# Attention rows of one core: transposing by pairs of heads over two key tiles, into wide tiles, with four pairs of row buffers

## The chip, the core and the metric

The kernel runs on one core of a Trainium2 chip, in one launch. The metric is the device time of that launch in microseconds (us). The kernel before takes 1777.0 us, the median of three runs (1774.48 to 1779.74).

## What is computed

Two layers of a diffusion backbone over 512 latent tokens and 256 context tokens of width 1024. Layer 0 is windowed attention with 16 query heads and 4 key heads of 64, layer 1 is retention; each is followed by a gated feed-forward part. The change touches the attention of layer 0 alone. Cut to what matters, for each block `b` of 128 latent queries:

```python
s_ctx = einsum('bqkgd,bnkd->bkgqn', qb, k_c) * scale           # 256 context keys
s_loc = einsum('bqkgd,bnkd->bkgqn', qb, kb) * scale            # keys within 128 of the query
s_loc = where(valid, s_loc, NEG_INF)
p = softmax(concatenate([s_ctx, s_loc, sink_col], -1))
o = einsum('bkgqn,bnkd->bqkgd', p[..., :L], v_c) + einsum('bkgqn,bnkd->bqkgd', p[..., L:L+band], vb)
out_x = o @ w_o
```

The context queries attend in the same way, to the context keys alone.

## The kernel before

Everything is fp32. Large products are made of three fp32r products each (`mm3`, lines 148 to 150). The attention of layer 0 is a double loop (lines 787 to 797): over the four groups `g` of one key head and four query heads, and inside over six blocks, the latent blocks 0 to 3 and the context blocks 0 and 1. A block is a call of `attend` and does this:

- `score(i)`, once for each of the four heads. PE multiplies 128 queries with the block's keys into a bank of PSUM (line 684; three banks). DVE adds the mask, writes the *row tile* `pr` (128 queries by up to 640 keys and one sink column) and keeps the row's extreme (line 685). POOL has written the sink column (line 668), which is the first write to that row tile. After the second head of a pair DVE makes the two biases (691), ACT the two exponentials with their sums (101), DVE the reciprocals (695), and POOL scales the two row tiles (698).
- `turn(ki)`, once for each key tile of 128 keys (4, 5, 5, 4 tiles for the latent blocks, 2 for a context block). PE transposes that tile of all four heads into one of two PSUM banks `pT` (707), in the order of heads 0, 2, 1, 3. ACT copies it to a tile `tt` of 512 columns where `ki` is even, DVE where it is odd (709).
- `output()`. For each key tile two products of the values with 256 columns of `tt` (719). Its first product waits for the block's last copy, so that all run together. The result goes to `o_raw` (734) or, in the last group, is split into `h` tiles (165, 166).

There are seven row buffers (`PRB`), and six buffers of `tt` (`TTB`). Before the loop both are also used in making the keys: `kn` (line 513) are `tt` tiles, `ksq` and a temporary of `key_factor` are `pr` tiles, and `rope_key` (520) takes one more `tt`.

Between the blocks of one group the query projections of the next are made (`make_q`, called in line 791); they are 96 products per pair of heads that depend on no softmax. After the loop come the output weights (`wo`, lines 809 to 824): each tile of 1024 weights is loaded, split by ACT into `whi` (140) and by DVE into `wlo` (141), and multiplied. The first two output tiles need only latent blocks.

The order in which the instructions stand in each engine's queue is not the program's. Outside the stretches under `manual_schedule` a scheduler decides it when the kernel is built: it takes what its own model holds ready, and by the program's order between those. On the chip each engine then works through its fixed queue. POOL's queue holds lines 668, 698 and 570 (a step of `make_q`), SP's the loads.

Of the kernel before, what the change touches and what calls it, by code (L numbers as in the profile page):

```python
# [14 lines left out]
P = 128  # L15
# [26 lines left out]
N_SMALL = C_C + 16  # L42

NM = 7
PRB = 7
TTB = 6


@with_exitstack
def dit_kernel(ctx, tc, xT, cT, crow, small, consts, masks, tabs0, tabs1, jtab, adaQ, adaN, adaT, wst, out):  # L50
    nc = tc.nc
# [10 lines left out]
    def T(pool, cols, tag, bufs, dt=F32):  # L62
        return pool.tile([P, cols], dt, tag=tag, bufs=bufs, name=tag)
# [8 lines left out]
    ident, bd = cst[:, 0:128], cst[:, 128:256]  # L72
# [16 lines left out]
    turn = {"pre": None, "lnexp": [], "silu": []}  # L89
# [418 lines left out]
    ap = At.enter_context(tc.tile_pool(name="ap", bufs=1, reuse_waits="tile"))  # L508
# [1 line left out]


    kx, kc = {}, {}
    kn = [T(ap, 512, "tt", TTB) for _ in range(3)]
    ksq = [T(ap, 656, "pr", PRB)[:, :512] for _ in range(3)]
    off_grid(ap, 16)
    for a, b, o in zip(kn, ksq, (kvx[0], kvc, kvx[1])):
# [2 lines left out]

    def rope_key(t):  # L520

        yy = T(ap, 512, "tt", TTB)
        nc.vector.stream_shuffle(yy, t, swap16)
        nc.vector.tensor_tensor(t, t, rope0[:, 0:512], op=mult)
        nc.vector.tensor_tensor(yy, yy, rope0[:, 512:1024], op=mult)
        nc.vector.tensor_tensor(t, t, yy, op=add)
# [18 lines left out]
    q, stats = {}, {}  # L545

    def make_q(j, raw=None):

        w = next_w(ap, 1, raw)
        qs = T(ap, 64, "qs", 4)[:, 0:36].rearrange("p (f n) -> p f n", f=3)
        sqs, o = [], [None, None]

        def part(s, k0, k1):
            if k0 == 0:
                o[s] = pj(NTOK[s])
            for k in range(k0, k1):
                mm3(o[s], (w[0][:, k * P:(k + 1) * P], w[1][:, k * P:(k + 1) * P]), h[s][k], k == 0, k == KT - 1)

        def shape(s):
            n = NTOK[s]
            sq, qn = t_sq(n), t_hn(n)
            nc.scalar.activation(qn, o[s], AF.Identity, scale=qk_gain[:, 0:1])
            nc.scalar.activation(sq, o[s], AF.Square)
            sqs.append(sq)
            if s == 0:
                sw = t_y(s)
                nc.vector.stream_shuffle(sw, qn, swap16)
                nc.gpsimd.tensor_tensor(qn, qn, rope0[:, 0:512], op=mult)  # L570
                nc.vector.tensor_tensor(sw, sw, rope0[:, 512:1024], op=mult)
                nc.vector.tensor_tensor(qn, qn, sw, op=add)
            qa = T(ap, 512, "q", 9, F32R)
            if s == 0:
                qb = T(ap, 512, "q", 9, F32R)
            else:
                qa, qb = qa[:, 0:SC], qa[:, SC:2 * SC]
            nc.scalar.copy(qa[0:64, :], qn[0:64, :])
            nc.scalar.copy(qb[64:128, :], qn[64:128, :])
            nc.vector.tensor_tensor(qa[64:128, :], qn[0:64, :], qa[0:64, :], op=sub)  # L580
            nc.vector.tensor_tensor(qb[0:64, :], qn[64:128, :], qb[64:128, :], op=sub)
            q[2 * j, s] = qa
            q[2 * j + 1, s] = qb

        def norms():
            tot = pj(12)
            for s, sq in enumerate(sqs):
                for b in range(NTOK[s] // P):
                    c = 8 * s + 2 * b
                    nc.tensor.matmul(tot[:, c:c + 2], sq[:, b * P:(b + 1) * P], bd[:, 0:P:64], start=True, stop=True)  # L590
            y, u, z = qs[:, 0], qs[:, 1], qs[:, 2]
            neg_half_rstd(y, z, tot, HD)
            nc.vector.scalar_tensor_tensor(u, tot, HD * EPS, y, add, mult)
            ue = u.rearrange("p (b e) -> p e b", e=2)
            for e in range(2):
                hd = 2 * j + e
                nc.vector.tensor_scalar(ue[:, e], ue[:, e], nsink[:, hd:hd + 1], -4.0 / HD, op0=mult, op1=mult)
                stats[hd] = qs

        def first():  # L600
            part(0, 0, 5)

        def second():
            part(0, 5, KT)
            shape(0)
            part(1, 0, 3)

        def third():
            part(1, 3, KT)
            shape(1)  # L610

        return [first, second, third, norms]
# [36 lines left out]
    class Block:  # L649


        def __init__(self, g, s, b):
            self.g, self.s, self.b = g, s, b
            self.lk = list(range(max(0, b - 1), min(4, b + 2))) if s == 0 else []
            ck = [4, 5]
            self.keys = ck + self.lk if s == 0 and b == 3 else self.lk + ck
            self.pr = []

        def score(self, i):
            g, s, b, n = self.g, self.s, self.b, len(self.keys) * P  # L660
            hd, nl = 4 * g + i, len(self.lk) * P
            if i % 2 == 0:
                self.st = T(ap, 16, "stat", 4)
            st, c = self.st, 2 * (b + 4 * s)
            qt = q[hd, s][:, b * P:(b + 1) * P]
            pt = T(ap, 656, "pr", PRB)[:, :n + 1]
            top = stats[hd][:, 1, c + hd % 2:c + hd % 2 + 1]
            nc.gpsimd.tensor_copy(pt[:, n:n + 1], top)
            lo, x0 = st[:, i % 2:i % 2 + 1], self.lk[0] * P if nl else 0

            if nl == 384:
                runs = [(nl, SC, 5 * P, [(0, SC, kc)]), (0, nl, 2 * P, [(0, nl, kx)])]
            elif nl == 0:
                runs = [(0, SC, 5 * P, [(0, SC, kc)])]
            elif b == 0:
                runs = [(0, n, 3 * P, [(0, nl, kx), (nl, SC, kc)])]
            else:
                runs = [(0, n, 0, [(0, SC, kc), (SC, nl, kx)])]
            for c0, w, m0, parts in runs:
                bank = pS()[:, :w]  # L680
                for p0, pw, kk in parts:
                    for r in range(2):
                        keys = kk[g][r] if kk is kc else kk[g][r][:, x0:x0 + pw]
                        nc.tensor.matmul(bank[:, p0:p0 + pw], qt, keys, start=r == 0, stop=r == 1)  # L684
                nc.vector.tensor_tensor_reduce(pt[:, c0:c0 + w], bank, mask[:, m0:m0 + w], 1.0, top, add, ALU.min, lo)  # L685
                top = lo
            self.pr.append(pt)
            if i % 2 == 0:
                return
            y = stats[hd][:, 0, c:c + 2]  # L690
            nc.vector.scalar_tensor_tensor(st[:, 2:4], st[:, 0:2], -1.0, y, mult, mult)  # L691
            for e in range(2):
                pt = self.pr[i - 1 + e]
                lnexp(pt, pt, AF.Exp, scale=y[:, e:e + 1], bias=st[:, 2 + e:3 + e], accum_out=st[:, 4 + e:5 + e])
            nc.vector.reciprocal(st[:, 6:8], st[:, 4:6])  # L695
            for e in range(2):
                pt = self.pr[i - 1 + e]
                nc.gpsimd.tensor_scalar(pt[:, :n], pt[:, :n], st[:, 6 + e:7 + e], 1.0, op0=mult, op1=mult)  # L698
            if i == 3:
                self.tt = []  # L700

        def turn(self, ki):
            if ki >= len(self.keys):
                return
            tp = pT()
            for a in range(4):
                nc.tensor.transpose(tp[:, a * P:(a + 1) * P], self.pr[(0, 2, 1, 3)[a]][:, ki * P:(ki + 1) * P], ident)  # L707
            tt = T(ap, 512, "tt", TTB)
            self.last = nc.scalar.copy(tt, tp) if ki % 2 == 0 else nc.vector.tensor_copy(tt, tp)
            self.tt.append(tt)  # L710

        def output(self):
            g, s, b = self.g, self.s, self.b
            O = pO()[:, :256]
            for ki, (t, tt) in enumerate(zip(self.keys, self.tt)):
                vg = vt[t][:, g * HD:(g + 1) * HD]
                f, l = ki == 0, ki == len(self.keys) - 1
                for e in range(2):
                    ins = nc.tensor.matmul(O[64 * e:64 * e + 64, :], vg, tt[:, 256 * e:256 * e + 256], start=f, stop=l)  # L719
                    if f:  # L720
                        tc.add_manual_dep(ins.ins, self.last.ins.name, run_dep, reason="value products in one run")
            if g == NKV - 1:
# [10 lines left out]
            dst = o_raw[g, s, b // 2].rearrange("p (e b q) -> p e b q", e=2, b=2)[:, :, b % 2, :]  # L733
            nc.vector.tensor_copy(dst, O.rearrange("p (e q) -> p e q", e=2))

    def attend(g, s, b):
        blk = Block(g, s, b)
        for i in range(4):
            blk.score(i)
        for ki in range(len(blk.keys)):  # L740
            blk.turn(ki)
        blk.output()

    def split_o(g):
# [65 lines left out]
    for d4 in range(0, KT, 4):  # L810
# [3 lines left out]
        for s, res in ((0, xr), (1, cres)):  # L814
            for d in range(d4, d4 + 4):
                o = pj(NTOK[s])
                project(w[d - d4], o_t[s], o)
                ins = gated_add(s, 0, 2, d, o, res)
# [236 lines left out]
    f, prev = 0, None  # L1055
    for gsz in FFN_GROUPS:
        acts = []
        for i in range(gsz):
# [4 lines left out]
            else:  # L1063
                if f == PLAIN:
                    last_sum()
                a, end = seven()
# [563 lines left out]
    f, prev = 0, None  # L1630
# [160 lines left out]
```

## Time and profile before

| what | value |
|---|---|
| median of three runs | 1777.0 us (1774.48 to 1779.74) |
| profiled execution | 1777.24 us, span of its instructions 1775.5 us |
| PE, DVE, ACT, POOL busy in the span | 97%, 76%, 47%, 8% |
| granted TensorE clock, mean | 0.994 |
| stage of the attention blocks | about 102 to 326 us |

The profiled execution's own time is 1.7 us over its span and 0.2 us over the median. "Busy" of PE counts matmuls whose ends are modelled, and they overlap, so that a short wait may not show as idle time. In the lists below a line reads: group, count, busy time, mean duration in ns, then the idle time of the engine just before the group and what ended it. A line of the timeline reads: start, duration, engine, source line, operation, tiles, shape, count, and in brackets the idle time before it with what ended it.

### The profile page before, as it was taken

How to read it: one execution, taken by the hardware profiler on the slowest of the kernel's cores; microseconds unless marked ns; L12 is line 12 of the kernel's file. 1: busy time of each engine (PE TensorE's matmuls, PEld its weight loads, DVE VectorE, ACT ScalarE, POOL GpSimd, SP SyncE). 2: the span in 40 equal slices, each digit the busy share in tenths (PEclk: the TensorE clock that was granted, in tenths of full speed). 3: DMA queues.
4: the chain of work that ended last, by engine and by line, in shares of the span. 5: the costliest groups of instructions: out<-in, count | busy, mean ns of one | idle time of the engine just before them, and what ended most of it. 6: DMA issues, size and time to landing. Idle time of an engine off the chain costs nothing.

```text
span 1775.5 us, 27602 instructions
## 1 busy us (share of the span) xinstructions
PE 1717.1 (97%) x10852; PEld 1527.1 (86%) x10852; DVE 1356.0 (76%) x2365; ACT 841.2 (47%) x1477; POOL 134.4 (8%) x275
## 2 busy tenths in 40 slices
PE   6899999999999999999998999999999999999999
PEld 4777776789999999999978788898897899999998
DVE  6697786788778778777789758758758798777774
ACT  5477676456333434242465534524524564445432
POOL 0035344100000000000010000000000000000000
PEclk9999999999999999999999999999999999999999
DMA  8610002434243534343342534434433323333222
GB/s 334 239 36 25 25 1 84 145 107 165 73 154 107 157 116 143 119 146 111 123 133 88 164 106 132 153 102 132 153 104 119 95 72 116 94 112 107 92 88 83
DMA packets 59891, 206.68 MB, mean 116 GB/s; under 512 B 6641, under 2 KB 7025, under 8 KB 59505
## 3 DMA queue, kind: packets, MB, share of 16 engines
q1 hardware_dynamic: 52848, 179.75, 31.2%
q0 software_dynamic: 6912, 25.17, 4.8%
q8 instruction: 85, 1.39, 0.3%
q14 instruction: 46, 0.37, 0.1%
HBM read 202.80 MB, written 2.10 MB: 115 GB/s over the span
## 4 chain that ended last, share of the span: by engine, by line
PE 74%; DVE 13%; ACT 4%; DMA 4%; issue 2%; POOL 2%; SPq 0%; ACTq 0%; DVEq 0%; POOLq 0%
PE Y L835 13%; PE Z L835 6%; PE pj L148 6%; PE pj L150 6%; PE pj L149 6%; PE Y L1180 4%; PE Z L1193 3%; PE X L835 3%; DVE wlo L166 3%; DMA wraw<-in_wst_dram 2%; PE pT L707 2%; PE S L684 2%; PE pO L719 2%; PE pj L1193 2%; PE X L1180 1%
## 5 line engine op out<-in xcount | busy, mean ns | idle before, releaser
L165 ACT CAST whi<-wraw 128x1024 fp32r<-128x1024 f32 x177 | 185.5, 1051 | 305.3 <-PE Z L150 71.5
L166 DVE TENSOR_TENSOR wlo<-wraw,whi 128x1024 fp32r<-128x1024 f32 x177 | 215.7, 1221 | 42.1 <-ACT whi L165 41.6
L835 PE MATMUL Y<-aq,whi 128*128 128x384 f32 x640 | 173.7, 335 | 0.9 <-ACT hn L973 0.8
L253 DVE SCALAR_TENSOR_TENSOR res<-pj,mod,res 128x512 f32<-128x512 f32 (+1 forms) x112 | 81.6, 729 | 70.3 <-PE pj L150 69.1
L141 DVE TENSOR_TENSOR wlo<-wraw,whi 128x1024 fp32r<-128x1024 f32 x80 | 97.9, 1223 | 36.6 <-ACT whi L140 36.0
L140 ACT CAST whi<-wraw 128x1024 fp32r<-128x1024 f32 x80 | 84.0, 1050 | 75.9 <-DMA wraw<-in_wst_dram 26.8
L835 PEld LDWEIGHTS Y<-aq,whi 128*128 128x128 f32 x640 | 116.6, 188 | 2.4 <-ACT hn L973 2.0
L271 DVE CUSTOM_DVE_ANT_0 y<-adaw,crow,small_sb 128x1024 bf16<-128x1024 f32 x64 | 81.9, 1279 | 33.7 <-DMA adaw<-in_adaT_dram 33.5
L835 PE MATMUL Y<-aq,wlo 128*128 128x384 f32 x320 | 107.0, 334 | 0.0
L101 ACT ACTIVATE pr<-pr,stat,qs 128x513 f32<-128x513 f32 (+2 forms) x96 | 74.2, 775 | 30.7 <-DVE stat L691 29.8
L1193 PE MATMUL Z<-whi,sA 128*128 128x512 f32 x256 | 81.0, 392 | 0.6 <-ACT whi L165 0.6
L698 POOL TENSOR_SCALAR pr<-pr,stat 128x512 f32<-128x512 f32 (+2 forms) x96 | 68.0, 721 | 86.7 <-DVE stat L695 66.6
L148 PE MATMUL pj<-ax,whi 128*128 128x512 f32 x176 | 68.7, 390 | 1.0 <-DVE res L253 1.0
L150 PE MATMUL pj<-ax,whi 128*128 128x512 f32 x176 | 68.6, 390 | 0.0
L149 PE MATMUL pj<-ax,wlo 128*128 128x512 f32 x176 | 68.5, 389 | 0.0
L707 PE MATMUL pT<-const_sb,pr 128*128 128x128 f32 x352 | 58.0, 284 | 10.9 <-POOL pr L698 8.6
L148 PE MATMUL pj<-act,whi 128*128 128x512 f32 x168 | 66.0, 393 | 0.1
L149 PE MATMUL pj<-act,wlo 128*128 128x512 f32 x168 | 65.9, 392 | 0.0
L707 PEld LDWEIGHTS pT<-const_sb,pr 128*128 128x128 f32 x352 | 38.8, 140 | 31.3 <-POOL pr L698 19.2
L150 PE MATMUL pj<-act,whi 128*128 128x512 f32 x168 | 65.5, 390 | 0.0
L268 POOL DMA_DIRECT2D adaw<-in_adaT_dram x48 | 25.6, 533 | 520.6 <-DVE mod L271 420.8
L685 DVE CUSTOM_DVE_ANT_0 pr<-S,mask,qs 128x256 f32<-128x256 f32 (+1 forms) x96 | 53.1, 567 | 14.3 <-PE S L684 7.9
(518 smaller groups left out, 5273.7 us busy)
## 6 DMA issues: line engine op xcount, KB each, us to landing
wraw<-in_wst_dram SPq DMA_DIRECT2D x238, 512.0 KB, 3.6
adaw<-in_adaT_dram POOLq DMA_DIRECT2D x48, 512.0 KB, 3.9
wx<-in_wst_dram SPq DMA_DIRECT2D x24, 512.0 KB, 4.6
adan<-in_adaQ_dram SPq DMA_DIRECT2D x16, 512.0 KB, 8.0
adan<-in_adaN_dram SPq DMA_DIRECT2D x16, 512.0 KB, 8.5
res<-in_xT_dram SPq DMA_DIRECT2D x16, 256.0 KB, 5.5
adaw<-in_adaT_dram SPq DMA_DIRECT2D x8, 512.0 KB, 4.0
aq<-in_adaN_dram SPq DMA_DIRECT2D x12, 256.0 KB, 6.4
```

The costliest lines, as they stand in the source:

```text
L140: nc.scalar.copy(hi, raw)
L141: nc.vector.tensor_tensor(lo, raw, hi, op=sub)
L148: nc.tensor.matmul(o, whi, xhi, start=first, stop=False)
L149: nc.tensor.matmul(o, wlo, xhi, start=False, stop=False)
L150: return nc.tensor.matmul(o, whi, xlo, start=False, stop=last)
L165: nc.scalar.copy(hi, t)
L166: return nc.vector.tensor_tensor(lo, t, hi, op=sub)
L271: after(nc.vector.tensor_tensor_reduce(junk, w, cr[:, s * 1024:(s + 1) * 1024], 1.0, sm_t[:, C_ADAB + l * 48 + j:C_ADAB + l * 48 + j + 1], ...
L707: nc.tensor.transpose(tp[:, a * P:(a + 1) * P], self.pr[(0, 2, 1, 3)[a]][:, ki * P:(ki + 1) * P], ident)
L835: nc.tensor.matmul(o, p, r, start=first and k + i == 0, stop=k == 3 and i == 2, skip_group_check=not first)
L1180: ins = nc.tensor.matmul(o[:, e * SC:(e + 1) * SC], p[:, ws], r, start=first and k + e + i == 0, stop=k == 3 and i == 2, skip_group_check= ...
L1193: ins = nc.tensor.matmul(o, p, r, start=first and k + i == 0, stop=k == 3 and i == 2, skip_group_check=not first)
```

## The change

`turn` takes two key tiles and two heads at a time instead of one key tile and four heads; `tt` tiles are 1024 columns wide, three of them instead of six of 512; there are eight row buffers instead of seven.

- A wide tile holds two key tiles of all four heads: the first pair of heads in its left half, the second pair in its right half. `turns` goes over the first pair with all whole pairs of key tiles, then over the second pair. Where the number of key tiles is odd, the last one is turned for all four heads together as before.
- The copy of the 1st, 3rd bundle of a pair of heads is ACT's, that of the 2nd DVE's, and the odd last tile's ACT's. Over all blocks ACT has 56 copies instead of 48, DVE 32 instead of 40. Counts of transposes (352), value products (176), row tiles (96) and POOL's scalings (96) stay.
- `moving` picks from a wide tile the 256 columns of a key tile and a head of each pair: two runs of 128 columns that lie 512 apart. Before they were 256 columns in a row.
- `kn` are the left halves of the three wide tiles; the temporary of `rope_key` becomes a row buffer. A tile `qs` shrinks from 64 to 48 columns.

```diff
-PRB = 7
-TTB = 6
+PRB = 8
+TTB = 3
...
-    kn = [T(ap, 512, "tt", TTB) for _ in range(3)]
+    kn = [T(ap, 1024, "tt", TTB)[:, :512] for _ in range(3)]
...
     def rope_key(t):
-        yy = T(ap, 512, "tt", TTB)
+        yy = T(ap, 656, "pr", PRB)[:, :512]
...
-        def turn(self, ki):
-            if ki >= len(self.keys):
-                return
+        def turn(self, kis, heads, eng):
             tp = pT()
-            for a in range(4):
-                nc.tensor.transpose(tp[:, a * P:(a + 1) * P], self.pr[(0, 2, 1, 3)[a]][:, ki * P:(ki + 1) * P], ident)
-            tt = T(ap, 512, "tt", TTB)
-            self.last = nc.scalar.copy(tt, tp) if ki % 2 == 0 else nc.vector.tensor_copy(tt, tp)
-            self.tt.append(tt)
+            for i, (ki, hd) in enumerate((ki, hd) for ki in kis for hd in heads):
+                nc.tensor.transpose(tp[:, i * P:(i + 1) * P], self.pr[hd][:, ki * P:(ki + 1) * P], ident)
+            while len(self.tt) <= kis[0] // 2:
+                self.tt.append(T(ap, 1024, "tt", TTB))
+            dst = self.tt[kis[0] // 2][:, heads[0] * 256:heads[0] * 256 + 512]
+            self.last = nc.scalar.copy(dst, tp) if eng == 0 else nc.vector.tensor_copy(dst, tp)
+
+        def turns(self):
+            n = len(self.keys)
+            for p in range(2):
+                for ki in range(0, n - 1, 2):
+                    self.turn((ki, ki + 1), (2 * p, 2 * p + 1), ki // 2 % 2)
+            if n % 2:
+                self.turn((n - 1,), (0, 1, 2, 3), 0)
+
+        def moving(self, ki, e):
+            n, t = len(self.keys), self.tt[ki // 2]
+            if n % 2 and ki == n - 1:
+                return t[:, 0:512].rearrange("p (j e q) -> p e j q", j=2, e=2)[:, e]
+            return t.rearrange("p (j k e q) -> p k e j q", j=2, k=2, e=2)[:, ki % 2, e]
...
-                    ins = nc.tensor.matmul(O[64 * e:64 * e + 64, :], vg, tt[:, 256 * e:256 * e + 256], start=f, stop=l)
+                    ins = nc.tensor.matmul(O[64 * e:64 * e + 64, :], vg, self.moving(ki, e), start=f, stop=l)
...
-        for ki in range(len(blk.keys)):
-            blk.turn(ki)
+        blk.turns()
```

The scheduler places all instructions of the stage anew. On PE the queue is the same up to the first transposes and again from the last value product on; ACT's, DVE's and POOL's come together again there. On SP the load of one tile of output weights moves from before the twelve loads of the residual streams to behind them.

More of the change, by code (lines that the diff above doesn't have):

```diff
@@ L551, in make_q @@
         w = next_w(ap, 1, raw)
-        qs = T(ap, 64, "qs", 4)[:, 0:36].rearrange("p (f n) -> p f n", f=3)
+        qs = T(ap, 48, "qs", 4)[:, 0:36].rearrange("p (f n) -> p f n", f=3)
         sqs, o = [], [None, None]
@@ L656, in __init__ @@
             self.keys = ck + self.lk if s == 0 and b == 3 else self.lk + ck
-            self.pr = []
+            self.pr, self.tt = [], []
         def score(self, i):
@@ L698, in score @@
                 nc.gpsimd.tensor_scalar(pt[:, :n], pt[:, :n], st[:, 6 + e:7 + e], 1.0, op0=mult, op1=mult)
-            if i == 3:
-                self.tt = []
-        def turn(self, ki):
-            if ki >= len(self.keys):
-                return
-            tp = pT()
-            for a in range(4):
-                nc.tensor.transpose(tp[:, a * P:(a + 1) * P], self.pr[(0, 2, 1, 3)[a]][:, ki * P:(ki + 1) * P], ident)
-            tt = T(ap, 512, "tt", TTB)
-            self.last = nc.scalar.copy(tt, tp) if ki % 2 == 0 else nc.vector.tensor_copy(tt, tp)
-            self.tt.append(tt)
+        def turn(self, kis, heads, eng):
+            tp = pT()
+            for i, (ki, hd) in enumerate((ki, hd) for ki in kis for hd in heads):
[16 more added lines that the diff above has]
+            return t.rearrange("p (j k e q) -> p k e j q", j=2, k=2, e=2)[:, ki % 2, e]
         def output(self):
@@ L714, in output @@
             O = pO()[:, :256]
-            for ki, (t, tt) in enumerate(zip(self.keys, self.tt)):
+            for ki, t in enumerate(self.keys):
                 vg = vt[t][:, g * HD:(g + 1) * HD]
```

## The prediction

> **What bounds the kernel now.** I read the page first, then the busy times by stretch.
>
> ```profile
> span 1775.5 us, 27602 instructions
> PE 1717.1 (97%) x10852; PEld 1527.1 (86%) x10852; DVE 1356.0 (76%) x2365; ACT 841.2 (47%) x1477; POOL 134.4 (8%) x275
> ```
> ```profile
> 102.00:326.00 224.00, 210.28 (x1445) 162.47 (x1444) 172.94 (x543) 152.49 (x360) 91.81 (x199) 1.00 0.11 37
> 326.00:1775.00 1449.00, 1426.26 (x8522) 1298.78 (x8522) 1116.00 (x1663) 636.43 (x1020) 38.32 (x65) 0.99 0.38 119
> ```
>
> PE bounds the program. The change lies in the first stretch, where PE is idle for 224.0 - 210.3 = 13.7 us (columns: stretch, length, then PE, PEld, DVE, ACT, POOL). Behind it PE is 98% busy and the queues are the same in both kernels, so what the stage gains or loses reaches the end. The list of waits in this stage says what PE waits for, and what waits for PE (us in total, times, longest):
>
> ```profile
> POOL pr L668 <- PE pT L707: 29.2, 18, 3.5
> ...
> PE pT L707 <- POOL pr L698: 8.6, 14, 1.2
> ...
> PE pT L707 <- ACT tt L709: 1.3, 4, 0.4
> ```
>
> Two thirds of PE's idle time stands before a transpose whose row tile POOL has not scaled yet. And 18 times POOL's first write to a row tile waited for transposes: with seven buffers, the fourth head of a block reuses one of the block before, and all four heads' buffers are freed by the last key tile. One such loop, at the fourth latent block of group 2, in the timelines of PE, POOL and DVE:
>
> ```profile
> 252.39 0.91 PE L707 MATMUL pT<-const_sb,pr 128*128 128x128 f32 x5
> ...
> 252.86 0.54 POOL L668 COPY pr<-qs 128x1 f32<-128x1 f32 x4 [1.55 <-PE pT L707]
> ...
> 252.87 0.75 DVE L685 CUSTOM_DVE_ANT_0 pr<-S,mask,qs 128x512 f32<-128x512 f32 x1
> ...
> 254.57 1.77 DVE L571 TENSOR_TENSOR y<-y,rope 128x512 f32<-128x512 f32 x1
> ...
> 257.87 0.15 DVE L695 RECIPROCAL stat<-stat 128x2 f32<-128x2 f32 x1
> ...
> 258.12 1.88 POOL L698 TENSOR_SCALAR pr<-pr,stat 128x512 f32<-128x512 f32 x2 [2.33 <-DVE stat L695]
> ...
> 258.96 0.55 PE L707 MATMUL pT<-const_sb,pr 128*128 128x128 f32 x3 [1.13 <-POOL pr L698]
> ```
>
> The last transposes of one block at 252.4 let the fourth row of the next be written at 252.9; its scaling comes at 258.1, and PE stands still.
>
> **The change part by part.** *The loop goes.* With eight buffers a block's rows reuse those of the block before last, and a first pair is freed before the second. Of the 14 waits, four are not of the loop (their fourth row was written before the other heads' work was through, or there was no block before):
>
> ```profile
> 112.36 0.44 PE L707 MATMUL pT<-const_sb,pr 128*128 128x128 f32 x2 [0.42 <-POOL pr L698]
> ...
> 195.40 0.55 PE L707 MATMUL pT<-const_sb,pr 128*128 128x128 f32 x3 [0.20 <-POOL pr L698]
> ...
> 272.29 0.66 PE L707 MATMUL pT<-const_sb,pr 128*128 128x128 f32 x4 [1.23 <-POOL pr L698]
> ...
> 322.22 1.11 PE L707 MATMUL pT<-const_sb,pr 128*128 128x128 f32 x6 [0.39 <-POOL pr L698]
> ```
>
> 8.6 - (0.42 + 0.20 + 1.23 + 0.39) = 6.4 us may go: I take -6.4. The bounds are 0 (the reciprocal of the example also stood behind other DVE work) and -8.6.
>
> *A first pair of heads gets a wait of its own.* Before, the first transposes of a block needed heads 0 and 2 and the rest all four; now 24 blocks have two such points each. In the built queue of the second latent block of groups 1 and 2 there stand, between the last scores of head 1 and that pair's first transposes, the scores of two heads, eight transposes, eight value products and four projection products. Rows of these kinds, and the chain of a pair of 640 columns (mean ns behind the bar's comma):
>
> ```profile
> 289.75 0.48 PE L684 MATMUL S<-kc,q 128*128 128x256 f32 x2
> ...
> 290.43 0.39 PE L684 MATMUL S<-kc,q 128*128 128x256 f32 x2
> ...
> 292.09 0.40 PE L148 MATMUL pj<-h,whi 128*128 128x512 f32 x1
> ...
> 292.33 0.40 PE L149 MATMUL pj<-h,wlo 128*128 128x512 f32 x1
> ...
> 294.87 1.04 PE L707 MATMUL pT<-const_sb,pr 128*128 128x128 f32 x8
> ...
> 297.78 2.38 PE L719 MATMUL pO<-tt,v 128*64 128x256 f32 x20
> ```
> ```profile
> L101 ACT ACTIVATE pr<-pr,stat,qs 128x641 f32<-128x641 f32 x32 | 29.4, 920 | 21.7 <-DVE stat L691 21.6
> ...
> L698 POOL TENSOR_SCALAR pr<-pr,stat 128x640 f32<-128x640 f32 x32 | 26.9, 853 | 40.4 <-DVE stat L695 26.3 <-DVE stat L691 14.1
> ...
> L685 DVE CUSTOM_DVE_ANT_0 pr<-S,mask,qs 128x256 f32<-128x256 f32 x64 | 29.8, 478 | 10.1 <-PE S L684 5.4 <-PE pT L707 4.3
> ...
> L685 DVE CUSTOM_DVE_ANT_0 pr<-S,mask,stat 128x384 f32<-128x384 f32 x32 | 19.2, 606 | 0.7 <-PE S L684 0.2
> ```
>
> PE's cover, from start to start since matmuls overlap (a head's scores run from its context product to the next head's), is 2 x (290.43 - 289.75) + 1.04 + 8 x 2.38 / 10 (a value product is two instructions, so x20 are ten) + 4 x (292.33 - 292.09) = 5.3 us. The chain is 0.48 + 0.61 for the mask, 2 x 0.92 for the exponentials, 2 x 0.85 for the scalings and about 0.3 for biases and reciprocal (0.15 each, as at 257.87): 4.9 us, without any queue on the way. So the new points are tight, and queues make some of them wait. Queued behind a waiting transpose is all of PE. No row shows such a point; the nearest are the old ones, 8.6 / 24 = 0.36 us for a block. 24 new ones would cost 8.6; a second pair is scored ahead of the first pair's transposes, so a wait for the first lets the second run on, and I take half: +4.3 (0 to +8.6).
>
> *The end of the stage.* The last head of the last context block, before (PE, DVE and POOL):
>
> ```profile
> 317.15 0.48 PE L684 MATMUL S<-kc,q 128*128 128x256 f32 x2
> ...
> 318.24 0.47 DVE L685 CUSTOM_DVE_ANT_0 pr<-S,mask,qs 128x256 f32<-128x256 f32 x1
> ...
> 321.36 0.15 DVE L695 RECIPROCAL stat<-stat 128x2 f32<-128x2 f32 x1
> ...
> 321.69 0.93 POOL L698 TENSOR_SCALAR pr<-pr,stat 128x256 f32<-128x256 f32 x2 [3.56 <-DVE stat L695]
> ...
> 324.20 1.08 PE L719 MATMUL pO<-tt,v 128*64 128x256 f32 x8 [0.88 <-ACT sq L209]
> ...
> 326.59 0.80 PE L148 MATMUL pj<-h,whi 128*128 128x512 f32 x1 [1.30 <-ACT whi L140]
> ```
>
> In the built queues of the change no copy of DVE stands ahead of this mask, the reciprocal stands ahead of the splits, and four projection products stand between the last transposes and the value products, where PE now idles 0.88 us for the copy. I take 0.9 for the copy, and 0.9 for mask and reciprocal (the mask begins 318.24 - 317.63 = 0.6 after the scores' end): -1.8, bounds 0 and -2.5. The 1.30 us before the next product stays: ACT splits those weights behind the block's result in both queues.
>
> *Banks.* Four waits of 1.3 us for a bank's copy: bundles of one pair come with other work between in the last blocks; half, -0.7 (bounds -1.3 and 0).
>
> *The clock.* PE's granted clock falls once in the stage. Stretches of 3.41 us there, and elsewhere (the last three numbers are clock, DMA share and GB/s):
>
> ```profile
> 323.13:326.54 3.41, 1.28 (x10) 0.57 (x8) 1.68 (x3) 2.24 (x5) 0.00 (x0) 1.00 1.01 412
> 326.54:329.95 3.41, 3.04 (x6) 2.11 (x7) 2.56 (x3) 3.38 (x5) 0.00 (x0) 0.50 0.89 292
> 329.95:333.37 3.42, 3.42 (x9) 2.65 (x8) 1.29 (x2) 2.29 (x3) 0.00 (x0) 0.50 0.64 247
> 903.40:906.80 3.40, 1.62 (x14) 1.42 (x13) 3.40 (x7) 2.21 (x5) 1.51 (x2) 1.00 0.25 55
> 906.80:910.20 3.40, 2.51 (x10) 1.76 (x11) 3.40 (x5) 1.04 (x3) 1.75 (x1) 1.00 0.54 146
> ```
>
> After 1.28 us of work in 3.41 the clock is halved for 6.8 us; after 1.62 it is not. Half of 3.04 + 3.42 is 3.2; less 0.3 for waits that would show again, 2.9. Without the 0.88 before the value products a stretch there keeps 1.28 + 0.88 = 2.2 us of work, over 1.62: I take -2.9 (bounds 0 and -3.2). The Trainium skill's page "TensorE: Matmul & The Clock Gate", section "What's actually happening", has the clock halved after at least one idle window of about 3.4 us. The row at 323.13 differs, since PE worked in it. By the rule alone this fall would not hang on the 0.88 us, and the sum would lack this term: 1772.4.
>
> *What costs nothing.* Eight copies go from DVE to ACT, which is idle for a third of the stage. The value products read two runs of 128 columns instead of one of 256; two products of 256 columns (0.39 at 290.43) take no longer than one of 512 (0.40 at 292.09), so not even a new start shows: 0, and no gain is possible as the columns are the same. The load that moves behind twelve others on SP brings weights that are split only at the stage's end; cover lost, it would add to the wait at 326.59. POOL's queue keeps its instructions, in another order. The keys' temporaries end before the first scores, under projections.
>
> The sum: -6.4 + 4.3 - 1.8 - 0.7 - 2.9 = -7.5, on the profiled execution's 1777.24 us: 1769.7. The median lies 0.2 lower: **1769.5 us**.
>
> **The rivals.** *The waits change place.* What the loop gives back, the first pairs take (+6.4 instead of +4.3), and the clock falls as before: -1.8 - 0.7 - 0.2 = 1774.3. For it: cover 5.3 against chain 4.9. Against: 18 blocked writes go for certain. Chance 0.28.
>
> *Slower: POOL stays late, and is asked twice.* DVE's addition at 254.57 took 1.77 us and POOL's two scalings of 512 columns 1.88, while two engines were at work on the same memory. If rows come as late as now because of that, nothing of the 8.6 goes, the 24 new points cost their 8.6 in full, and the end gains 1.8: 1777.0 + 6.8 = 1783.8. It decides from where the first pairs' waits pass 6.4 + 5.3 us. For it: only 4 of 24 blocks are in the loop with more than 1 us. Chance 0.22. The Trainium skill's page "SBUF — State Buffer", section "Who interferes with whom", speaks for it: a DVE operation with two SBUF inputs and POOL exclude each other for a whole instruction.
>
> *Slower: wide tiles run out.* A block of five key tiles holds all three, the old six buffers left one. At the two changes to a next block of four or five key tiles in each group, PE would wait for a bank for about a copy and half a bundle of eight (0.59 as ACT's tt copies, 1.04 / 2): 8 x 1.1 = 8.8, less 2.5: 1783.3. It needs transposes of the next block ahead of this block's value products; the built queue has them behind. Chance 0.05.
>
> ```profile
> L709 ACT COPY tt<-pT 128x512 f32<-128x512 f32 x48 | 28.1, 585 | 28.6 <-PE pT L707 28.1
> ```
>
> **How the numbers follow.** The forecast has 0.45, the rivals 0.28, 0.22 and 0.05. 0.3%, about what a measurement of this kernel can tell from no change, is 5.3 us: below 1771.7 or above 1782.3. The forecast is faster, the first rival within, the others slower: 0.45, 0.28, 0.27. The forecast's own range goes from all of 8.6, 2.5, 1.3 and 3.2 gained, cut by 5 for first pairs that must wait somewhere, 1766, to no gain of the clock, 1772.4. If first pairs never wait it is near 1761. The range of 8 in 10 reaches from 1760 to 1784.
>
> **What would show it.** Right: POOL's writes at L668 no longer wait for transposes; PE's waits for POOL total 4 to 7 us, at twice as many points; the value products of the last block wait for nothing; the clock stays at 1.00 around 326 us. Wrong: waits for POOL over 12 us, above all before first pairs; PE waiting for copies by more than 3 us; a stage that ends at 326 or later.

## The result, and the profile after

The changed kernel takes 1769.0 us, the median of 6 executions (1767.17 to 1771.39), against 1776.7 us before (6 executions): a ratio of 0.9952, 95% interval 0.9941 to 0.9963. The forecast was 1769.5. Two of the 6 stand on record with the same time, span and clock (1767.17 us), as if one execution had been listed twice; counted once, the median is 1769.9. The profiled execution took 1767.17 us, with a span of 1765.4 us.

From the page of the changed kernel, and the busy times by stretch (stretch, length, then PE, PEld, DVE, ACT, POOL; the last three numbers are granted clock, DMA share and GB/s):

```profile
span 1765.4 us, 27623 instructions
PE 1713.7 (97%) x10852; PEld 1526.2 (86%) x10852; DVE 1347.7 (76%) x2357; ACT 845.4 (48%) x1485; POOL 139.0 (8%) x275
```
```profile
102.00:326.00 224.00, 214.14 (x1463) 166.87 (x1462) 167.78 (x539) 161.44 (x374) 95.39 (x196) 1.00 0.14 46
326.00:1765.00 1439.00, 1417.49 (x8498) 1292.34 (x8496) 1112.10 (x1658) 631.42 (x1013) 38.70 (x65) 1.00 0.38 118
```

PE has as much to do as before. In the first 224 us of the stage it idles 9.9 us where it idled 13.7, and has got 18 instructions further. The list of waits in the stage, as shown of before, with three lines added that matter now (us in total, times, longest):

```profile
POOL pr L668 <- PE pT L704: 22.7, 23, 1.7
...
PE pT L704 <- POOL pr L698: 3.8, 10, 1.0
...
PE pj L148 <- ACT whi L140: 2.0, 2, 1.4
PE pT L704 <- DVE tt L708: 2.0, 2, 1.0
...
DVE pr L685 <- PE pT L704: 0.9, 2, 0.4
```

And the same line of before as the last one:

```profile
DVE pr L685 <- PE pT L707: 5.9, 8, 0.9
```

PE's waits for POOL fall from 8.6 to 3.8 us. The waits for a bank's copy were 1.3 us, on ACT; now they are 2.0 us, on DVE. POOL's first writes to row tiles (668) still wait for transposes, 23 times instead of 18: that sign was read wrongly. What has all but gone (5.9 us to 0.9) is the wait behind them, that of a mask (685) for a row tile that transposes still held.

The end of the stage, in PE's timeline after, and below it one row of before that stands for the same product as the last of after:

```profile
316.70 1.08 PE L731 MATMUL pO<-tt,v 128*64 128x256 f32 x8
319.18 0.49 PE L148 MATMUL pj<-h,whi 128*128 128x512 f32 x1 [1.40 <-ACT whi L140]
320.29 0.50 PE L148 MATMUL pj<-h,whi 128*128 128x512 f32 x1 [0.62 <-ACT whi L140]
...
323.37 0.39 PE L149 MATMUL pj<-h,wlo 128*128 128x512 f32 x1
```
```profile
333.40 0.39 PE L149 MATMUL pj<-h,wlo 128*128 128x512 f32 x1
```

The first product behind the stage starts at 319.18 where it was 326.59: 7.4 us earlier. Of these 0.95 stood already at 63 us, ahead of the change (PE's first product stood at 12.56 in this execution and at 13.59 in the one before), so 6.5 are the stage's. At 323.37 the lead is 10.0 us: the kernel before ran these products at half the clock. At the end of the program it is 10.1. The two profiled executions lie apart by more than the medians, 7.7.

### The profile page after: what moved, and what is told of

It reads as the page before. It is cut to its first block, busy times and chain, and to the rows that moved or that the text cites. A ratio compares the mean times of both kernels' runs of the same rounds, so it can differ in the third digit from the quotient of the medians.

```text
span 1765.4 us, 27623 instructions
## 1 busy us (share of the span) xinstructions
PE 1713.7 (97%) x10852; PEld 1526.2 (86%) x10852; DVE 1347.7 (76%) x2357; ACT 845.4 (48%) x1485; POOL 139.0 (8%) x275
## 4 chain that ended last, share of the span: by engine, by line
PE 76%; DVE 13%; ACT 4%; DMA 4%; issue 2%; POOL 1%; SPq 0%; ACTq 0%; DVEq 0%; POOLq 0%
PE Y L846 14%; PE Z L846 7%; PE pj L149 6%; PE pj L150 6%; PE pj L148 6%; PE Y L1191 4%; PE X L846 3%; PE Z L1204 3%; DMA wraw<-in_wst_dram 2%; DVE wlo L166 2%; PE pT L704 2%; PE pO L731 2%; PE pj L1204 2%; PE S L684 1%; PE X L1191 1%
```

## How the executions were compared

The executions of one kernel differ by 2.5 to 7 us, nearly as much as the change is worth, and about two fifths of that scatter (in variance) goes with the granted clock, which is listed for each. Over 111 executions of eleven kernels (the doubled one counted once) I fitted the span as a constant for each kernel plus a common slope on (1 - mean granted clock) x span. The slope is 0.37 (standard error 0.05): clock that is lost costs about a third of itself. That part of it falls into PE's waits would explain this, and no run isolates it; the one fall followed above, of 6.8 us at half the clock, cost 2.6 of the 3.4 us lost. The constants (standard errors of their differences 0.5 to 0.7 us) compare kernels at one clock. The runs come in three batches from two chips; before's median is 1777.9 to 1778.0 in each. This is arithmetic on the listed numbers, and the clock is listed to three digits only (1.8 us).

| kernel | median us | ratio to before, 95% | PE's waits for POOL in the stage, us | mean clock | at one clock, us against before |
|---|---|---|---|---|---|
| before (42 executions) | 1778.0 | | 8.6 | 0.9929 | 0 |
| changed (6, then 5; 10 in the last two columns) | 1769.0, 1768.7 | 0.9952; 0.9947 [0.9933, 0.9961] | 3.8; 3.9 | 0.9962 | -6.6 |
| buffers8 | 1769.6 | 0.9951 [0.9938, 0.9963] | 3.4 | 0.9952 | -7.1 |
| pairs7 | 1771.2 | 0.9963 [0.9950, 0.9975] | 6.0 | 0.9950 | -5.2 |
| alternate | 1771.8 | 0.9965 [0.9954, 0.9977] | 5.6 | 0.9948 | -5.1 |
| wide7 | 1774.9 | 0.9989 [0.9980, 0.9998] | 6.9 | 0.9939 | -1.5 |
| before_ahead | 1773.8 | 0.9974 [0.9965, 0.9984] | 7.6 | 0.9946 | -3.0 |
| casts_ahead | 1769.3 | 0.9948 [0.9935, 0.9960] | 3.9 | 0.9960 | -7.4 |
| ahead_act | 1767.8 | 0.9938 [0.9924, 0.9952] | 4.3 | 0.9958 | -9.3 |
| rope_dve | 1770.2 | 0.9955 [0.9941, 0.9970] | 8.7 | 0.9952 | -6.4 |
| rope_dve_8 | 1766.2 | 0.9930 [0.9917, 0.9943] | 3.6 | 0.9944 | -11.4 |

The scheduler places the stage's queues anew for each of these kernels except before_ahead and casts_ahead, whose queues on PE and POOL are those of their base. A difference of 1 or 2 us between the others is therefore an edit together with a placement.

## Experiments

**The changed kernel again**, without an edit.

> The changed kernel once more, beside the others, as their common base. Theory (the clock's fall at the stage's end hangs on where the 3.41 us stretches of the clock happen to lie): PE's work in the worst stretch of 3.41 us there is 1.40 us in the changed kernel (from 316.9) and 1.24 in the one before (from 323.2), both under 1.5, so in the changed kernel too some executions, about one in three, lose 2.7 to 3.2 us there, and spans scatter over 3 to 4 us. Rival (my prediction's: the fall is gone because the value products no longer wait): no execution has it, and spans scatter by 1 us or less. Median of the time 1768 to 1770 by the first, 1767 by the second.

Measured: 1768.7 us; the second profile has no fall of the clock at the stage's end either. Spans go from 1766.3 to 1768.8. That settles neither theory: there is no fall in two profiles, where the first theory has one in three, and the spans scatter by 2.5 us, where the second has 1. The median lies in the first theory's range. The mean clock is the clearer sign: 0.9929 over 42 executions of before and 0.9962 over 10 of the changed kernel. Times the spans that is 12.6 against 6.7 us of lost clock, at the slope 0.37 a gain of 2.2 us.

**Which part pays: the buffers, the order by pairs, the wide tiles.** Three kernels with one part each, and one that takes the order away.

buffers8, on the kernel before:

```diff
-PRB = 7
+PRB = 8
...
-        qs = T(ap, 64, "qs", 4)[:, 0:36].rearrange("p (f n) -> p f n", f=3)
+        qs = T(ap, 48, "qs", 4)[:, 0:36].rearrange("p (f n) -> p f n", f=3)
```

> The kernel before with eight row buffers in place of seven and nothing else of the change (a small tile shrinks to make room). Theory (the loop of row buffers): POOL's first writes to row tiles hardly wait for transposes any more (29.2 us before), PE's waits for POOL in the stage fall from 8.6 to 2 or 3 us, and the time falls by 4 to 6 us, to 1771 to 1773. Rival (the order by pairs does it, the buffers only follow): PE's waits for POOL stay over 6 us and the time falls by less than 2 us.

Measured: 1769.6 us, as fast as the whole change, and about twice the gain that the theory gave. Its waits in the stage, and PE's one wait for weights at the stage's end:

```profile
POOL pr L668 <- PE pT L707: 32.9, 21, 4.0
...
PE pT L707 <- POOL pr L698: 3.4, 8, 0.8
```
```profile
PE pj L149 <- DVE wlo L141: 0.6, 1, 0.6
```

PE's waits for POOL fall as far as with the whole change, while POOL's own waits at 668 do not fall at all (29.2 before). No wait of a mask for transposes is listed any more. So the theory's effect on PE came, and its sign did not. I take the mask that cannot start for the link, and POOL's longer waits to be for rows that are needed a block later; that is argued, not shown. The mask alone does not order the kernels: alternate below lists no such wait and PE waits 5.6 us for POOL, rope_dve lists 2.8 us and PE waits 8.7. Nor is all of the gain the loop's: at the stage's end, 0.9 us ahead of the last value products and 1.6 for weights became the 0.6 us shown, with the new placement of the queues.

pairs7, on the changed kernel:

```diff
-PRB = 8
+PRB = 7
```

> The changed kernel with seven row buffers. Theory (the loop of row buffers): where a block has an even number of key tiles its first pair is freed half a block earlier, where it has five the last tile still frees all four heads at once; so POOL's writes wait again in the eight blocks of five tiles, PE's waits for POOL are 2 to 4 us over those of the changed kernel (3.8), and the time is 1 to 3 us over it. Rival (the order by pairs alone does it): the same time as the changed kernel within 1 us.

Measured: 1771.2 us, 2.5 over the changed kernel. In the list of waits:

```profile
PE pT L704 <- POOL pr L698: 6.0, 11, 1.2
...
DVE pr L685 <- PE pT L704: 1.5, 3, 0.6
```

As the theory has it, 2.2 us of waits come back. Both this kernel and buffers8 gain most of the whole, and the two gains do not add up. That fits the theory's account, in which the order by pairs frees buffers early and the eighth buffer makes that unnecessary; pairs7 has the wide tiles and a placement of its own besides.

alternate, on the changed kernel (the two loops of `turns` change places):

```diff
-            for p in range(2):
-                for ki in range(0, n - 1, 2):
-                    self.turn((ki, ki + 1), (2 * p, 2 * p + 1), ki // 2 % 2)
+            for ki in range(0, n - 1, 2):
+                for p in range(2):
+                    self.turn((ki, ki + 1), (2 * p, 2 * p + 1), ki // 2 % 2)
```

> The changed kernel with the bundles of the two pairs in turn (first two key tiles of pair 0, then of pair 1, then the next two), in place of all of pair 0 ahead of pair 1. Eight row buffers, wide tiles and bundles by two key tiles stay; what goes is that the first pair is through, and freed, before the second is needed. Theory (eight buffers are enough by themselves, as buffers8 showed, and the order by pairs adds little): within 2 us of the changed kernel, 1768 to 1771; PE's waits for POOL 3 to 6 us. Rival (the order by pairs has a part of its own that eight buffers do not give): 3 us or more slower than the changed kernel, with PE's waits for POOL over 7 us.

Measured: 1771.8 us, with waits for POOL of 5.6 us and for ACT's copies of 3.3 us:

```profile
PE pT L704 <- POOL pr L698: 5.6, 12, 1.1
PE pT L704 <- ACT tt L708: 3.3, 3, 1.4
```

This lies between the two theories. The time is 3.1 over the changed kernel, as the rival has it, but only 1.5 of it at one clock, and the waits for POOL stay under 7 us. With wide bundles by two key tiles the order by pairs is worth 1.5 to 3 us, while buffers8, which has neither, is as fast as both together.

wide7, on the kernel before (with the edits of `TTB`, `kn` and `rope_key` as in the change):

```diff
-            tt = T(ap, 512, "tt", TTB)
+            self.wide = T(ap, 1024, "tt", TTB) if ki % 2 == 0 else self.wide
+            tt = self.wide[:, ki % 2 * 512:ki % 2 * 512 + 512]
```

> The kernel before with three tiles of 1024 columns in place of six of 512 and nothing else: transposes of one key tile for all four heads as before, seven row buffers; the value products read 256 columns in a row. Theory (wide tiles cost and bring nothing): the same as before within 0.1%, PE's waits for POOL 8 to 9 us, waits of PE for copies as before within 1 us. Rival (wide tiles run out): PE waits for copies by 5 us more, and the time is 1781 to 1786. Second rival (part of the gain is the wide tiles'): 2 us or more faster than before.

Measured: 1774.9 us, a ratio just under 1. PE waits 1.4 us for copies at transposes, as before (1.3): that wide tiles run out is refuted. The gain, 3.0 us in the median (as the second rival has it) and 1.5 at one clock, goes with 1.7 us less waiting for POOL (6.9). Whether the wide tiles or the new placement of the queues brings that is open.

**The end of the stage and the clock.** Two kernels in which ACT splits the weights of the next products first:

```diff
-        nc.scalar.copy(hi, raw)
+        cast.append(nc.scalar.copy(hi, raw))
...
-        nc.scalar.copy(hi, t)
+        late.append(nc.scalar.copy(hi, t))
...
+        [after(c, cast[-2:]) for c in late[-2:] if d4 == 0]
...
-                add_square(s, d, res[d])
+                after(add_square(s, d, res[d]), cast[-2:] if (s, d) == (0, 1) else [])
```

casts_ahead has this on the changed kernel:

> The changed kernel with ACT's two splits of output weights put ahead of the splits of the last block's result and of one square; the queues of PE and POOL stay as they are. PE's two waits at 319.2 and 320.3 (1.40 and 0.62 us) should go: the first split can start at 316.7, when ACT's last copy is through, so PE's next product stands at 317.8. Theory (the clock's stretches): 1.5 us are gained directly; the worst stretch of 3.41 us there then holds over 2.5 us of work, so no execution loses the clock there: 2.3 to 3 us less in the median than the changed kernel, and spans scatter less. Rival (clock not concerned): 1.5 us less and the same scatter. Third: the splits are held by something else (a load, a buffer), and nothing moves.

Measured: 1769.3 us against 1768.7, no gain in the median. In the profile the edit did what it should: PE's waits for these splits fall from 2.0 to 0.4 us, and behind them PE is 1.9 us ahead of the profile of "again", where it was 0.3 ahead before them: the 1.5 us expected came there. At the program's end 1.5 are left. At one clock the kernel is 0.8 us faster, about one standard error. Five executions do not tell, and the part of the theory on the clock is not borne out: the mean clock did not rise (0.9960).

before_ahead has the same edit on the kernel before:

> The kernel before with ACT's two splits of output weights put ahead of the splits of the last block's result and of one square, as in casts_ahead; the queues of PE and POOL stay as they are, and the loop of row buffers stays. It fills PE's waits at 326.6 and 327.7 (1.30 and 0.32 us), so the worst stretch of 3.41 us there holds over 2.5 us of PE's work in place of 1.24. Theory (the clock term is real: before lost the clock at the stage's end in most executions): no fall near 326 us, about 1.6 us less by the waits and 2.5 to 3 us less by the clock, a median 4 to 4.5 us under before. Rival (that fall was one execution's chance): 1.6 us less, no more.

Measured: 1773.8 us, 4.1 under before: the sum is as the first theory says, and its profile has no fall near 326 us (it has one at 235.5). The mean clock rises from 0.9929 to 0.9946, which is 3.1 us of lost clock, or about one stretch of 6.8 us at half speed in most executions; at the slope that is 1.1 us, and the other 3.0 are direct, where 1.6 were expected. So with PE's waits at this place some lost clock goes too, but it costs less than the 2.9 us of the prediction.

**Towards a faster kernel.** In the changed kernel two waits of 1.0 us, at 202.0 and 257.8, stand before transposes whose bank DVE has not copied. DVE's copy stood behind work that waited for POOL's step at line 570. ahead_act gives those copies to ACT, on casts_ahead:

```diff
-                    self.turn((ki, ki + 1), (2 * p, 2 * p + 1), ki // 2 % 2)
+                    self.turn((ki, ki + 1), (2 * p, 2 * p + 1), ki // 2 % 2 if self.b < 3 else 0)
```

> The changed kernel with the two splits ahead as in casts_ahead, and with all copies of the fourth latent block given to ACT, where PE waited 2 x 1.0 us at 202.0 and 257.8 for a copy that stood in DVE's queue behind work waiting for POOL, while ACT was idle. Theory: those two waits go and nothing takes their place: stage end 2 us earlier than in casts_ahead, 3.5 to 4 us earlier than in the changed kernel, time 1764 to 1766. Rival: ACT is late with the exponentials of the next block, and the waits come back as waits for POOL: no better than casts_ahead.

Measured: 1767.8 us. Yet the two waits stayed and changed their engine:

```profile
PE pT L704 <- POOL pr L698: 4.3, 10, 1.0
PE pT L704 <- ACT tt L708: 2.0, 2, 1.0
```

ACT's copy now stands in its queue behind a cast that waits for the same step of POOL. The mechanism of the theory failed; the gain of 0.9 us in the median to the changed kernel, 1.9 to casts_ahead at one clock, is not explained by it.

rope_dve gives that step to DVE, on casts_ahead; rope_dve_8 has it on buffers8 with the splits ahead, so with the turn and the tiles of before:

```diff
-                nc.gpsimd.tensor_tensor(qn, qn, rope0[:, 0:512], op=mult)
+                nc.vector.tensor_tensor(qn, qn, rope0[:, 0:512], op=mult)
```

> casts_ahead (the changed kernel with the two splits ahead) with the step of line 570, a product of 512 columns in the query projections, given from POOL to DVE. In ahead_act the two waits of 1.0 us stayed, since ACT's copies then stood behind a cast that waits for the same step on POOL (1.78 us at 198.5). Theory (what is left of the waits hangs on that step: it takes 1.60 us on POOL, and about 0.7 on DVE, which has a quarter of the stage idle): the two waits go and PE's waits for POOL fall below 3 us; the time is 2 to 4 us under the changed kernel, 1765 to 1767. Rival (DVE becomes late with masks and copies, the more so as its queue is placed anew): waits for copies and scores rise by what the others lose, and the time is that of casts_ahead or worse.

> The kernel before with eight row buffers (as buffers8), the two splits ahead and the step of line 570 on DVE: the turn and the tiles stay those of before. Theory (the row buffers are the gain, the order by pairs and the wide tiles add nothing that these two edits do not give as well): within 2 us of rope_dve. Rival (the order by pairs has its own part once the other waits are gone): over 2 us slower than rope_dve.

Measured: 1770.2 and 1766.2 us. PE's waits in the stage, first of rope_dve, then of rope_dve_8:

```profile
PE pT L704 <- POOL pr L698: 8.7, 12, 1.5
PE pj L149 <- DVE wlo L141: 0.4, 1, 0.4
PE pO L731 <- DVE tt L708: 0.3, 1, 0.3
```
```profile
PE pT L707 <- POOL pr L698: 3.6, 9, 0.8
PE S L684 <- DVE stat L685: 1.1, 3, 0.5
```

In both, the waits for copies at transposes are gone. With the order by pairs the waits for POOL come back to 8.7 us, so rope_dve gains nothing; why they do, no run isolates. With the old turn they stay at 3.6, and rope_dve_8 is the fastest kernel here: 0.9930 of before (0.9917 to 0.9943), against 0.9947 and 0.9952 for the changed kernel. So the theory for rope_dve fell and its rival was right on the time, though not on the cause (copies and scores do not wait more). For rope_dve_8 both theories were wrong: it is 4 us faster than rope_dve, which says that the order by pairs and the wide tiles are not needed.

## Why the prediction was right, and where not

**The stage decides, and the rest follows it.** Right: 6.5 us are won in the stage, and from 440 us on the lead stays between 9.9 and 11.4.

**The loop, -6.4.** Right in size. Of the ten waits for POOL that are left, three are a first pair's, and seven, 2.6 us, a second pair's. So the old points went from 8.6 to 2.6: -6.0. In the place that the prediction showed, the fourth row is now written at 234.7 at the latest, not at 252.9:

```profile
233.19 1.48 POOL L668 COPY pr<-qs 128x1 f32<-128x1 f32 x4
...
252.34 1.36 POOL L698 TENSOR_SCALAR pr<-pr,stat 128x512 f32<-128x512 f32 x2
```

Its pair is scaled at 252.34, and no wait for POOL follows there. The sign that the prediction named, "POOL's writes no longer wait", was wrong, as buffers8 shows; which wait behind them counted is argued above, not shown.

**First pairs, +4.3.** This step was mis-sized: all their waits are these three, 1.2 us, two of them in the very first block:

```profile
111.47 0.44 PE L704 MATMUL pT<-const_sb,pr 128*128 128x128 f32 x2 [0.41 <-POOL pr L698]
...
112.57 0.88 PE L704 MATMUL pT<-const_sb,pr 128*128 128x128 f32 x6 [0.43 <-POOL pr L698]
...
307.77 0.89 PE L704 MATMUL pT<-const_sb,pr 128*128 128x128 f32 x3 [0.35 <-POOL pr L698]
```

The row of the old points was the wrong neighbour. I read it so that those waited because their masks came late, which a first pair's do not; no run isolates that. The comparison of 5.3 us of cover with a chain of 4.9, made in the same paragraph, was the better evidence, and I set it aside.

**The end of the stage, -1.8.** The value products wait for nothing at 316.70, so 0.9 came as said. Of the 0.9 for mask and reciprocal, the wait of 0.39 us for POOL ahead of the last transposes is gone, which the 6.0 above already hold; the rest cannot be seen apart. The wait for the weights grew by 0.4 (1.6 to 2.0).

**Banks, -0.7.** Wrong in sign: ACT's 1.3 us went and 2.0 on DVE came, +0.7. I had not looked at what stands ahead of DVE's copies. The rival "POOL stays late, and is asked twice" had named the cause, though at another engine's expense:

```profile
254.67 1.51 DVE L166 TENSOR_TENSOR hc<-res,hc 128x256 fp32r<-128x256 f32 x1
...
257.04 0.68 DVE L708 COPY tt<-pT 128x512 f32<-128x512 f32 x1
...
258.44 0.43 DVE L166 TENSOR_TENSOR hc<-res,hc 128x256 fp32r<-128x256 f32 x1
```
```profile
254.11 1.78 POOL L570 TENSOR_TENSOR hn<-hn,rope 128x512 f32<-128x512 f32 x1 [0.41 <-DVE y L569]
```
```profile
257.76 0.66 PE L704 MATMUL pT<-const_sb,pr 128*128 128x128 f32 x4 [1.03 <-DVE tt L708]
```

The same DVE operation takes 0.43 us at 258.44 and 1.51 beside POOL's product, which it outlasts by 0.3; the copy follows it late, and PE waits. That roughly agrees with the rule of the Trainium skill's page "SBUF — State Buffer", section "Who interferes with whom", by which a DVE instruction with two SBUF inputs contends with one of POOL that reads SBUF, and the shared port pair is an exclusive lock. The wait does not hang on that, though: at 202.0 no such operation stands there, DVE's step at line 572 waits 1.17 us for POOL's product itself, and PE waits 0.97 us. (The prediction calls DVE's row at 254.57 an addition; line 571 is a product.)

**The clock, -2.9.** Between the two profiles it gave 2.6 us (the lead grows from 7.4 to 10.0), over all executions 2.2. The size was near. At the stage's end the reason given fits all twelve profiles, one or two of each kernel: the three in which PE waits there both ahead of the value products and for the weights (before 0.88 us, wide7 0.87, pairs7 0.67 ahead of the products) lost the clock there, the nine with one of these waits or none kept it. As a rule for other places it is not enough. The prediction took PE's busy time in a stretch as the measure, with a bound between 1.28 and 1.62 us. Stretches of the changed kernel, of before_ahead and of alternate:

```profile
315.46:318.87 3.41, 2.20 (x14) 1.08 (x12) 1.80 (x5) 2.58 (x5) 0.00 (x0) 1.00 0.95 388
318.87:322.28 3.41, 2.48 (x10) 1.87 (x11) 2.64 (x4) 3.38 (x5) 0.00 (x0) 1.00 0.93 377
```
```profile
232.04:235.46 3.42, 2.31 (x20) 2.03 (x19) 3.02 (x5) 2.62 (x7) 2.08 (x3) 1.00 0.00 0
235.46:238.87 3.41, 3.41 (x15) 3.23 (x16) 2.54 (x7) 1.69 (x5) 0.00 (x0) 0.50 0.00 0
```
```profile
147.45:150.87 3.42, 2.35 (x21) 2.15 (x20) 3.00 (x6) 2.51 (x6) 0.80 (x4) 1.00 0.01 2
150.87:154.28 3.41, 3.41 (x17) 2.24 (x18) 2.12 (x7) 1.69 (x3) 0.00 (x0) 0.50 0.02 5
```

The changed kernel kept its clock with 2.20 us, as predicted to the digit; but the others lost it after 2.31 and 2.35. The bound failed in the kernel before as well: there the clock fell at 1398.3 after a stretch with 1.67 us. And that 2.20 us stood in the stretch is partly luck, where the stretches fell: the emptiest 3.41 us there, from 316.9, hold 1.4.

**The sum.** -7.5 was forecast. The stage gave -6.5 and the clock -2.2 to -2.6, against -4.6 and -2.9. PE's listed waits from 102 to 330 us account for 5.2 of the 6.5 (13.8 to 8.6 us). The other 1.3 stand in no listed wait: from the first transposes to the first product behind the stage PE's idle time fell by 5.6 us and its busy time, over the same 1392 instructions, by 0.9. That the median came within 0.5 us of the forecast is partly luck, in two ways. Errors cancel in part: first pairs cost 3.1 us less than said and time in no listed wait 1.3 less, the loop gave 0.4 less, banks cost 1.4 more, the weights 0.4 more, and the clock gave up to 0.7 less. And the forecast stood on a base of 1777.0, of three runs, where 42 executions of before have 1778.0; against these, the 10 of the changed kernel (1769.1) gain 8.9 us, not 7.5.

## What to carry to other kernels

When an engine's first write to a buffer waits, look at who stands behind that write before counting the wait itself: here the waits stayed and the time went. Before a reordering is taken for the gain, try the one buffer more by itself; with the placement that came with it, it gave as much as the whole change. Where a queue order is built by a scheduler, two further edits were worth 3.4 us in the median on one base (1769.6 to 1766.2) and nothing on the other, so each must be measured on the base where it is to stay.

## What the runs showed of the hardware

A stretch can lose PE its clock though PE is shown busy for 2.31 of 3.42 us. Of that time 0.95 us are eight products of 2 columns (line 590), which occupy PE and stream next to nothing:

```profile
232.58 0.95 PE L590 MATMUL pj<-const_sb,sq 128*128 128x2 f32 x8
```

Without them it is 1.36 us, near the 1.28 of the stretch before 326.54 in the kernel before. So what PE streams fits the falls better than what it is busy; the exact measure is open (in rope_dve_8 the clock fell after a stretch of 2.34 us without such products). Counted from the shapes of the products that start in them, the two stretches hold 1,936 and 2,064 columns, that of rope_dve_8 2,560, that before 326.54 2,048, and the changed kernel's at 315.46, which kept its clock, 3,584; but one of before_ahead at 303.7, with 2,048 columns and 2.22 us, kept it too. Falls in the stage came at 235.5, 150.9, 277.6, 321.8 and, in wide7, 326.4 us, in single profiles of different kernels, at places where PE waits. The Trainium skill's page "TensorE: Matmul & The Clock Gate", section "What's actually happening", says that the window is free-running; the changing places agree with that, while no fall here needed a wholly idle window.
